# The end of FFN 1 in a one-layer encoder kernel: where weight copies, a table load, one tile's transposes and the next units stand

## The chip, the cores and the metric

The kernel runs on one core of one Trainium2 chip. A core has a matrix engine (TensorE, PE in the profile, with its weight loads as PEld), a vector engine (VectorE, DVE), a scalar engine (ScalarE, ACT), a general engine (GpSimd, POOL) and a queue engine (SyncE, SP); each works through its own list of instructions in order and waits on semaphores for the others. Data lies in SBUF, matmul results in PSUM banks, and 16 DMA engines move data from and to HBM.

The metric is the device time of one execution in microseconds (us). Before the change it is 1108.87 us, the median of three runs from 1108.83 to 1109.03.

## The reference

The reference computes one layer of a streaming encoder on 512 tokens of width 1024, in float32:

```python
h = x
f = swiglu(rms_norm(h, ffn1_pre_g), ffn1_w1, ffn1_w3, ffn1_w2)   # (silu(x@w1) * (x@w3)) @ w2, D_FF = 2816
h = h + 0.5 * rms_norm(f, ffn1_post_g)
u = rms_norm(h, mix_pre_g)
q, k, v, xr, xg = split(u @ w_in)                 # xr: 1024 columns
hr = rg_lru(causal_conv(xr))                      # gated linear recurrence over the tokens
y_a = (hr * gelu(xg)) @ w_lru_out
y_b = swa_sink_attention(q, k, v) @ w_attn_out    # windowed attention
g = sigmoid(u @ w_gate + b_gate)
h = h + rms_norm((g_a * y_a + g_b * y_b) @ w_o, mix_post_g)
h = h + 0.5 * rms_norm(swiglu(rms_norm(h, ffn2_pre_g), ffn2_w1, ffn2_w3, ffn2_w2), ffn2_post_g)
```

What matters here is the passage from the second line to the fifth: the end of FFN 1's last product, the norm of its result (post norm), the addition to `h`, the norm ahead of the mixer (pre norm), and the first products of `u` with the columns called `xr`.

## The kernel before

**Precision and matmuls.** Float32 products are made of three matmuls on split numbers: each operand is a high part (`whi`, a rounded copy) and a low part (`wlo`, the rest), and a product is high·high + high·low + low·high. So each weight tile of 128 x 1024 has to be copied (high part) and subtracted (low part) before PE can use it. For some weights, `xr` 0 to 3 among them, the low part is made by a DMA instead: ScalarE writes the negated high part (`wlo`, a second copy) and GpSimd issues a DMA that adds the weight from HBM to it. `dma_split(k, 0)` makes the first copy, `dma_split(k, 1)` the second and the DMA; `split_to` does both at once. `dma_to(n)` issues the plain loads (`raw_xr`) on SP's queue. Every instruction of an engine runs in the order in which the program writes it.

**The buffers.** All of these tiles come from one pool of 42 slots of 4 KB a partition; a new tile gets a slot that an older one has left, and its first writer waits for the older tile's last reader. PSUM has 8 banks, handed out in the same way.

**FFN 1's second product.** `tok_gemm` (called with `pre=half`) computes hidden @ w2 for four token tiles t = 0 to 3 of 128 tokens and two column halves n. Most of it is done by block products with sums of blocks (class `Halves`): seven products `m1, m5, m2, m6, m3, m7, m4` of five units each, 35 units u = 0 to 34 (`G` is 5). A unit has 12 matmuls of 512 columns, six for each token half. `step(u)` first prepares the operands of units up to u + 4 (`prep`: a ScalarE copy and a VectorE subtraction for the weight block at L686 and L694, the same for the hidden block at L226 and L227), then runs the unit's hooks, then issues its matmuls. At the end of `m7` (unit 29), VectorE adds the bank to a tile (L727), and only then may `m4` (units 30 to 34) go on in that bank. Two remaining rows of blocks (`TAIL_A`) are done as plain products, `classical(t, n)`, six matmuls each.

**The norms.** `norm(t, mid)` is post norm, addition and pre norm of one token tile: a chain between VectorE and ScalarE. VectorE adds the parts (L307) and scales (L310), ScalarE squares and sums (L309), the reciprocal root is taken on ScalarE with one correction on VectorE (L272 to L277), VectorE adds to `h` (L321), ScalarE squares again (L333), another root, and both engines scale one half of the result `hg` each (L344, L345). What `mid` issues stands between the first root and the second squares. After it, `transpose_mm` turns the tile by eight PE transposes (L354), and `transpose_out` writes its high part (ScalarE, L364) and low part (VectorE, L366) to `uT`, the operand of the next products. `transpose_xf` makes a float32 copy (L374) that is used later.

**The order at the end.** Units 0 to 24; tails of tiles 0 and 1; preparation to unit 31; norm 0; units 25 to 29 and the tails' column half 1 of tiles 2 and 3; preparation of units 33 and 34; norm 1; then, for tile 2: units 30 to 34 for token half 0, transposes of tile 0, the tail of tile 2, norm 2; for tile 3: units 30 to 34 for half 1, transposes of tile 1, the tail of tile 3. Then the first four units of the next product (`xr` 0 to 3, `bs[0]` to `bs[3]`): their first 256 tokens need tiles 0 and 1 alone, so `start` issues matmuls of 256 columns on those while norm 3 and the transposes of tiles 2 and 3 are made; the other 256 tokens come after that. Half of `bs[3]` is done with 512 columns at once.

**What stands in the hooks.** `X_AT` gives the units at which the plain loads of `xr` 0 to 3 are issued; the copies of `xr` 0 and 1 follow two units after their loads (`split_to`, ScalarE L159 and L160, GpSimd L161), those of `xr` 2 and 3 stand in the middles of norms 0, 1 and 2 (L169, L172, L174). `MARKS_A` gives the units for the loads and splits of the tails' weights and for the loads of `h` (L756, SP). `KEPT_AT` gives the units of three leftover gated products: scaling at units 15 and 16, `silu` at 18 and 19, product at 19 and 20. A root of a small tile is taken on ScalarE at unit 17 (`4 * G - 3`), so that the root's activation table is loaded there (L436). Each norm stores its `h` tile to HBM on SP's queue (L341).

Of the kernel before, what the change touches and what calls it, by code (L numbers as in the profile page):

```python
# [18 lines left out]
KT = D // P  # L19
# [32 lines left out]
def hybrid_layer(ctx: ExitStack, tc: tile.TileContext, a: dict, out: bass.AP):  # L52
# [111 lines left out]
    def dma_split(k, part):  # L164
        assert k == st["split"]
        if part == 0:
            dma_to(k + 1)
            half_split[k] = slot([P, D], F32R, name="whi"), slot([P, D], F32R, name="wlo")
            act.activation(half_split[k][0], raws[k], AF.Copy)  # L169
# [4 lines left out]
        pool.dma_start(out=lo, in_=a[nm][i * P : (i + 1) * P, :], accum_op=ALU.add)  # L174
        st["split"] += 1

    def split_to(n):
        while st["split"] < min(n, len(order)) and st["split"] not in paired:
            k = st["split"]
            dma_to(k + 1)  # L180
            r = raws.pop(k)
            if order[k] in BY_DMA:
                nm, i = order[k]
                pairs[k] = split_dma(r, a[nm][i * P : (i + 1) * P, :])
            else:
                hi = slot([P, D], F32R, name="whi")
                lo = slot([P, D], F32R, name="wlo")
                if order[k] in BY_POOL:
                    pool.tensor_copy(hi, r)
                else:  # L190
                    act.activation(hi, r, AF.Copy)
                dve.tensor_tensor(out=lo, in0=r, in1=f32(hi), op=ALU.subtract)
                pairs[k] = (hi, lo)
            st["split"] += 1
# [153 lines left out]
    def transpose_mm(hg):  # L348
        banks = []
        for half in range(2):  # L350
            ps = bank("tr")
            for k in range(4):
                kk = half * 4 + k
                pe.transpose(ps[:, k * P : (k + 1) * P], hg[:, kk * P : (kk + 1) * P], ident)  # L354
            banks.append(ps)
        return banks
# [20 lines left out]
    def tok_gemm(nm, xs, n, R, gpost_name, scale, gpre_name, first, x_to=None, xf=None, spill=False, then=None, eps=None, pre=None):  # L377
# [47 lines left out]
        def classical(t, n_):  # L425
            for k in tail:
                new = k == tail[0] and (t > 1 and n_ == 1 if pre else k == 0)
                mm_tok(accs(t), xs[k], t, w[k], new, k == tail[-1], (n_,), bool(pre))

        def norm(t, mid=None):  # L430
            us[t] = norms(acc[t], t, g[0], scale, g[1], spill, ep(t), mid, pre and pre.part(t), (1, 0) if pre and t > 1 else (0, 1))

        if pre:
            G = pre.G
            pre.hooks[3 * G].append(vectors)
            pre.hooks[4 * G - 3].append(lambda: act.activation(small(1, "tiny"), veps[:, 0:1], AF.Abs_reciprocal_sqrt))  # L436
# [24 lines left out]
            norm(1, lambda: [dma_split(x0 + 2, 1), dma_split(x0 + 3, 0)])  # L461
            for t in range(2, 4):
                for u in range(6 * G, 7 * G):
                    pre.step(u, (t - 2,))
                trs[t - 2] = transpose_mm(us[t - 2])
                transpose_out(trs[t - 2], t - 2, xf if t == 2 else None)
                classical(t, 0)
                if t == 2:
                    norm(2, lambda: dma_split(x0 + 3, 1))
            pre.bank.clear()  # L470
        else:
            tails()
            vectors()
            split_to(st["get"] + len(first))
            dma_to(st["split"] + 2)
            for t in range(NT):
                for n_ in range(2):
                    classical(t, n_)
                if t == NT - 1:
                    break  # L480
                if t >= 1:
                    trs[t - 1] = transpose_mm(us[t - 1])
                if t == NT - 2:
                    transpose_out(trs[t - 1], t - 1)
                norm(t)
                if t == 1:
                    transpose_out(trs[t - 1], t - 1, xf)
# [30 lines left out]
        k0, k1 = range(KT // 2), range(KT // 2, KT)  # L518
        whole = 3 if pre else 2
        mm_feat(bs[2], ws[2], 0, 256, ks=range(early, KT if pre else KT // 2))  # L520
        start(k0)
        get_ahead()
        for i in range(whole):
            mm_feat(bs[i], ws[i], 256, 512)
        if pre:
            point()
        mm_feat(bs[whole], ws[whole], 256, 512, ks=k0)
        if pre:
            point()
        mm_feat(bs[whole], ws[whole], ks=k1)  # L530
        if not pre:
            mm_feat(bs[3], ws[3])
        return bs

# [1393 lines left out]
```

## Time and profile before

| | |
|---|---|
| median of three runs | 1108.87 us (1108.83 to 1109.03) |
| the profiled execution, whole | 1109.03 us |
| its span, first to last instruction | 1107.2 us |
| PE busy in the span | 1092.7 us (99%) |
| DVE busy | 936.5 us (85%) |
| ACT busy | 700.8 us (63%) |
| POOL busy | 406.6 us (37%) |
| mean granted PE clock | 0.997 |

How to read the profile: it is one execution, with times in us from the first instruction of the span. A row of a timeline has start, duration, engine, line of the kernel, operation, `out<-in` by the program's tile names, shapes and a count; in brackets stands how long the engine was idle before it and what ended that wait. The wait table has, for an engine and line and what it waited for: us in total, times, longest. In the table of stretches each engine has its busy time and instructions, then come the granted PE clock (1.00 is full), the busy share of the DMA engines and GB/s. Matmuls are pipelined, so the end of one is later than the start of the next; I use distances from start to start. Queue engines have a `q` behind their name.

### The profile page before, as it was taken

The numbers are of one execution on the slowest core, as the hardware profiler recorded it, in microseconds if no ns is written. First come the engines' busy times: TensorE is split into PE (matmuls) and PEld (weight loads), VectorE is DVE, ScalarE is ACT, GpSimd is POOL, SyncE is SP. The second block draws the span as 40 slices with busy tenths as digits, with TensorE's granted clock in tenths as the row PEclk, the third lists the DMA queues.
The fourth block names the chain that finished last, engine by engine and source line by source line (L and its number), as shares of the span: only waits on it lengthen the run. The fifth ranks groups of instructions, "written<-read, shape, count | busy, mean of one in ns | idle before, by whom it ended". The sixth has DMA issues, their size and how long they took to land.

```text
span 1107.2 us, 18059 instructions
## 1 busy us (share of the span) xinstructions
PE 1092.7 (99%) x6850; PEld 987.9 (89%) x6850; DVE 936.5 (85%) x1328; ACT 700.8 (63%) x1211; POOL 406.6 (37%) x338
## 2 busy tenths in 40 slices
PE   9999999999989999999999999999999999999997
PEld 7899999988868877899888888888999999998886
DVE  5988999989888998888677867767789989999995
ACT  7756555598867687756656564456555555567672
POOL 0144923233001523223556564010877656521000
PEclk9999999999999999999999999999999999999999
DMA  9335653389856653147222245342423323547642
GB/s 337 121 84 138 136 142 115 124 180 203 244 144 189 179 127 114 41 148 251 78 76 85 90 170 209 127 183 81 143 76 115 102 90 111 195 149 187 179 120 90
DMA packets 53479, 156.99 MB, mean 142 GB/s; under 512 B 5504, under 2 KB 7424, under 8 KB 53392
## 3 DMA queue, kind: packets, MB, share of 16 engines
q1 hardware_dynamic: 43280, 129.57, 34.5%
q0 software_dynamic: 9824, 25.74, 12.2%
q8 instruction: 54, 0.88, 0.3%
q10 hardware_dynamic: 288, 0.52, 0.1%
q14 instruction: 33, 0.27, 0.1%
HBM read 137.99 MB, written 13.62 MB: 137 GB/s over the span
## 4 chain that ended last, share of the span: by engine, by line
PE 96%; DVE 1%; ACT 1%; issue 0%; DMA 0%; DVEq 0%; ACTq 0%
PE c L833 13%; PE c L834 13%; PE c L835 13%; PE f L237 10%; PE f L239 9%; PE f L238 9%; PE hw L717 5%; PE hw L715 5%; PE hw L716 5%; PE acc L255 1%; PE acc L256 1%; PE acc L257 1%; PE pt L1687 1%; PE s L1651 1%; PE s L1650 1%; PE o L1703 1%
## 5 line engine op out<-in xcount | busy, mean ns | idle before, releaser
L834 PE MATMUL c<-uT,wlo 128*128 128x256 f32 x516 | 146.1, 283 | 0.0
L835 PE MATMUL c<-uT,whi 128*128 128x256 f32 x516 | 146.1, 283 | 0.0
L833 PE MATMUL c<-uT,whi 128*128 128x256 f32 x516 | 146.1, 283 | 0.0
L833 PE MATMUL c<-Xh,whi 128*128 128x256 f32 x504 | 142.8, 283 | 0.0
L834 PE MATMUL c<-Xh,wlo 128*128 128x256 f32 x504 | 142.7, 283 | 0.0
L237 PE MATMUL f<-uT,whi 128*128 128x512 f32 (+1 forms) x376 | 138.0, 367 | 1.8 <-ACT uT L364 1.8
L239 PE MATMUL f<-uT,whi 128*128 128x512 f32 (+1 forms) x376 | 136.3, 363 | 0.2 <-DVE uT L366 0.2
L238 PE MATMUL f<-uT,wlo 128*128 128x512 f32 (+1 forms) x376 | 136.3, 362 | 0.0
L835 PE MATMUL c<-Xl,whi 128*128 128x256 f32 x456 | 129.1, 283 | 0.0
L227 DVE TENSOR_TENSOR wlo<-S,whi 128x1024 fp32r<-128x1024 f32 x86 | 121.0, 1408 | 5.9 <-POOL OL L1723 3.1
L226 ACT ACTIVATE whi<-S 128x1024 fp32r<-128x1024 f32 x86 | 88.5, 1054 | 29.7 <-DVE S L882 28.0
L833 PEld LDWEIGHTS c<-uT,whi 128*128 128x128 f32 x516 | 99.1, 192 | 0.2
L834 PEld LDWEIGHTS c<-uT,wlo 128*128 128x128 f32 x516 | 99.1, 192 | 0.2
L835 PEld LDWEIGHTS c<-uT,whi 128*128 128x128 f32 x516 | 99.1, 192 | 0.0
L833 PEld LDWEIGHTS c<-Xh,whi 128*128 128x128 f32 x504 | 96.8, 192 | 0.3 <-issue 0.3
L834 PEld LDWEIGHTS c<-Xh,wlo 128*128 128x128 f32 x504 | 96.8, 192 | 0.0
L717 PE MATMUL hw<-whi,uT 128*128 128x512 f32 x228 | 88.8, 390 | 0.0
L715 PE MATMUL hw<-whi,uT 128*128 128x512 f32 x228 | 88.7, 389 | 0.0
L716 PE MATMUL hw<-wlo,uT 128*128 128x512 f32 x228 | 88.7, 389 | 0.0
L835 PEld LDWEIGHTS c<-Xl,whi 128*128 128x128 f32 x456 | 87.6, 192 | 0.0
L237 PEld LDWEIGHTS f<-uT,whi 128*128 128x128 f32 x376 | 71.0, 189 | 14.4 <-ACT uT L364 2.2
L239 PEld LDWEIGHTS f<-uT,whi 128*128 128x128 f32 x376 | 70.9, 189 | 11.5 <-DVE uT L366 0.4
(441 smaller groups left out, 3193.7 us busy)
## 6 DMA issues: line engine op xcount, KB each, us to landing
raw_w2b<-in_w2b_dram SPq DMA_DIRECT2D x27, 512.0 KB, 4.6
raw_w1b<-in_w1b_dram SPq DMA_DIRECT2D x22, 512.0 KB, 4.2
raw_w3b<-in_w3b_dram SPq DMA_DIRECT2D x22, 512.0 KB, 4.4
raw_w3a<-in_w3a_dram SPq DMA_DIRECT2D x21, 512.0 KB, 4.7
raw_w1a<-in_w1a_dram SPq DMA_DIRECT2D x20, 512.0 KB, 4.3
raw_w2a<-in_w2a_dram SPq DMA_DIRECT2D x17, 512.0 KB, 8.3
raw_wg<-in_wg_dram SPq DMA_DIRECT2D x16, 512.0 KB, 4.0
raw_w2a<-in_w2a_dram POOLq DMA_DIRECT2D x15, 512.0 KB, 9.9
```

The lines of the kernel that those rows point to most:

```text
L226: act.activation(hi, src, AF.Copy)
L227: dve.tensor_tensor(out=lo, in0=src, in1=f32(hi), op=ALU.subtract)
L237: pe.matmul(ps[:, c0:c1], wh[:, s], h_, start=k == 0 and c0 == 0, stop=False, skip_group_check=True)
L238: pe.matmul(ps[:, c0:c1], wl[:, s], h_, start=False, stop=False, skip_group_check=True)
L239: pe.matmul(ps[:, c0:c1], wh[:, s], l_, start=False, stop=k == KT - 1, skip_group_check=True)
L255: pe.matmul(acc[n], x[:, 0, c], wh[:, s], start=first, stop=False, skip_group_check=skip)
L715: pe.matmul(ps, xs[:, 0, j, c], hi[:, j, :], start=start and j == 0, stop=False, skip_group_check=True)
L716: pe.matmul(ps, xs[:, 0, j, c], lo[:, j, :], start=False, stop=False, skip_group_check=True)
L717: pe.matmul(ps, xs[:, 1, j, c], hi[:, j, :], start=False, stop=i == self.G - 1, skip_group_check=True)
L833: pe.matmul(ps, wh[:, s], xh, start=first, stop=False, skip_group_check=True)
L834: pe.matmul(ps, wl[:, s], xh, start=False, stop=False, skip_group_check=True)
L835: pe.matmul(ps, wh[:, s], xl, start=False, stop=k == 3, skip_group_check=True)
```

## The change

It does five things at FFN 1's end; the second call of `tok_gemm` (without `pre`) keeps its order.

1. The copies of `xr` 0 and 1 leave the hooks. All copies of `xr` 0 to 3 are now issued around the norms: `xr` 0 (both copies) between the preparations and norm 0, `xr` 1 in the middle of norm 0, `xr` 2 between the preparations and norm 1, `xr` 3 with one copy in the middle of norm 1 and one in that of norm 2. All four low parts go by `dma_split`.
2. The plain loads of `xr` 0 to 2 are issued at units 22, 24 and 26 instead of 20, 21 and 24; that of `xr` 3 stays at 28.
3. The small root is taken at unit 22 (`4 * G + 2`), behind the last `silu` of unit 19, and not at unit 17.
4. After the transposes of tile 0 and the tail of tile 2, only unit 30 of token half 1 is done before the transposes of tile 1; then comes norm 2, and units 31 to 34 of half 1 and tile 3's tail follow. The float32 copies of tile 0 stand ahead of norm 2, those of tile 1 in its middle and behind it.
5. The first unit `bs[0]` is done whole for its first 256 tokens ahead of tile 2's transposes, `bs[1]` and `bs[2]` between those and tile 3's, `bs[3]` behind them; the second 256 tokens follow for all four, so that no matmul of these units has 512 columns.

```diff
-            pre.hooks[4 * G - 3].append(lambda: act.activation(small(1, "tiny"), veps[:, 0:1], AF.Abs_reciprocal_sqrt))
+            pre.hooks[4 * G + 2].append(lambda: act.activation(small(1, "tiny"), veps[:, 0:1], AF.Abs_reciprocal_sqrt))
...
             for i, u in enumerate(X_AT):
                 pre.hooks[u].append(lambda i=i: dma_to(x0 + i + 1))
-                if i < 2:
-                    pre.hooks[u + 2].append(lambda i=i: split_to(x0 + i + 1))
+
+            def x_split(i, parts=(0, 1)):
+                for p in parts:
+                    dma_split(x0 + i, p)
+
...
             pre.prep(5 * G + LEAD + 2)
-            norm(0, lambda: dma_split(x0 + 2, 0))
+            x_split(0)
+            norm(0, lambda: x_split(1))
...
-            norm(1, lambda: [dma_split(x0 + 2, 1), dma_split(x0 + 3, 0)])
-            for t in range(2, 4):
-                for u in range(6 * G, 7 * G):
-                    pre.step(u, (t - 2,))
-                trs[t - 2] = transpose_mm(us[t - 2])
-                transpose_out(trs[t - 2], t - 2, xf if t == 2 else None)
-                classical(t, 0)
-                if t == 2:
-                    norm(2, lambda: dma_split(x0 + 3, 1))
+            x_split(2)
+            norm(1, lambda: x_split(3, (0,)))
+            for u in range(6 * G, 7 * G):
+                pre.step(u, (0,))
+            trs[0] = transpose_mm(us[0])
+            transpose_out(trs[0], 0)
+            classical(2, 0)
+            pre.step(6 * G, (1,))
+            trs[1] = transpose_mm(us[1])
+            transpose_out(trs[1], 1)
+            transpose_xf(trs[0], 0, xf)
+            norm(2, lambda: [x_split(3, (1,)), transpose_xf(trs[1], 1, xf, (0,))])
+            transpose_xf(trs[1], 1, xf, (1,))
+            for u in range(6 * G + 1, 7 * G):
+                pre.step(u, (1,))
+            classical(3, 0)
...
         def between():
             transpose_out(trs[t - 1], t - 1, parts=(0,))
-            transpose_xf(trs[t - 2], t - 2, xf, (0,))
+            if not pre:
+                transpose_xf(trs[t - 2], t - 2, xf, (0,))
...
-        start(range(3))
-        trs[t - 1] = transpose_mm(us[t - 1])
-        mm_feat(bs[0], ws[0], 0, 256, ks=range(3, KT))
-        norm(t, between)
-        transpose_out(trs[t - 1], t - 1, parts=(1,))
-        transpose_xf(trs[t - 2], t - 2, xf, (1,))
-        start()
-        early = 5 if pre else 1
-        start(range(early))
+        if pre:
+            start()
+            trs[t - 1] = transpose_mm(us[t - 1])
+            norm(t, between)
+            transpose_out(trs[t - 1], t - 1, parts=(1,))
+            start()
+            start()
+        else:
...
-        mm_feat(bs[2], ws[2], 0, 256, ks=range(early, KT if pre else KT // 2))
-        start(k0)
+        if not pre:
+            mm_feat(bs[2], ws[2], 0, 256, ks=k0[1:])
+        start()
         get_ahead()
-        for i in range(whole):
-            mm_feat(bs[i], ws[i], 256, 512)
+        mm_feat(bs[0], ws[0], 256, 512)
+        mm_feat(bs[1], ws[1], 256, 512)
+        mm_feat(bs[2], ws[2], 256, 512, ks=k0)
         if pre:
+            mm_feat(bs[2], ws[2], 256, 512, ks=k1)
             point()
-        mm_feat(bs[whole], ws[whole], 256, 512, ks=k0)
-        if pre:
-            point()
-        mm_feat(bs[whole], ws[whole], ks=k1)
-        if not pre:
+            for ks in (k0, k1):
+                mm_feat(bs[3], ws[3], 256, 512, ks=ks)
+                point()
+        else:
+            mm_feat(bs[2], ws[2], ks=k1)
             mm_feat(bs[3], ws[3])
...
-X_AT = (20, 21, 24, 28)
+X_AT = (22, 24, 26, 28)
```

More of the change, by code (lines that the diff above doesn't have):

```diff
@@ L500, in between @@
             transpose_out(trs[t - 1], t - 1, parts=(0,))
-            transpose_xf(trs[t - 2], t - 2, xf, (0,))
-        start(range(3))
-        trs[t - 1] = transpose_mm(us[t - 1])
-        mm_feat(bs[0], ws[0], 0, 256, ks=range(3, KT))
-        norm(t, between)
-        transpose_out(trs[t - 1], t - 1, parts=(1,))
-        transpose_xf(trs[t - 2], t - 2, xf, (1,))
-        start()
-        early = 5 if pre else 1
-        start(range(early))
+            if not pre:
+                transpose_xf(trs[t - 2], t - 2, xf, (0,))
+        k0, k1 = range(KT // 2), range(KT // 2, KT)
+        if pre:
[6 more added lines that the diff above has]
+        else:
+            start(range(3))
+            trs[t - 1] = transpose_mm(us[t - 1])
+            mm_feat(bs[0], ws[0], 0, 256, ks=range(3, KT))
+            norm(t, between)
+            transpose_out(trs[t - 1], t - 1, parts=(1,))
+            transpose_xf(trs[t - 2], t - 2, xf, (1,))
+            start()
+            start(range(1))
         trs[t] = transpose_mm(us[t])
@@ L517, in tok_gemm @@
             then()
-        k0, k1 = range(KT // 2), range(KT // 2, KT)
-        whole = 3 if pre else 2
-        mm_feat(bs[2], ws[2], 0, 256, ks=range(early, KT if pre else KT // 2))
-        start(k0)
+        if not pre:
+            mm_feat(bs[2], ws[2], 0, 256, ks=k0[1:])
+        start()
         get_ahead()
-        for i in range(whole):
-            mm_feat(bs[i], ws[i], 256, 512)
+        mm_feat(bs[0], ws[0], 256, 512)
+        mm_feat(bs[1], ws[1], 256, 512)
+        mm_feat(bs[2], ws[2], 256, 512, ks=k0)
         if pre:
+            mm_feat(bs[2], ws[2], 256, 512, ks=k1)
             point()
-        mm_feat(bs[whole], ws[whole], 256, 512, ks=k0)
-        if pre:
-            point()
-        mm_feat(bs[whole], ws[whole], ks=k1)
-        if not pre:
+            for ks in (k0, k1):
[3 more added lines that the diff above has]
+            mm_feat(bs[2], ws[2], ks=k1)
             mm_feat(bs[3], ws[3])
```

## The prediction

> **What bounds the kernel now.** I read the page's first part, then who waited for whom on TensorE, then a table of stretches, then the timelines of each engine around FFN 1's end.
>
> ```profile
> PE 1092.7 (99%) x6850; PEld 987.9 (89%) x6850; DVE 936.5 (85%) x1328; ACT 700.8 (63%) x1211; POOL 406.6 (37%) x338
> ```
>
> TensorE (PE) is the bound: of a span of 1107.2 us it lacks 14.5. A change that takes no matmul away can win only waits, and this one works at the two largest.
>
> ```profile
> PE hw L715 <- DVE hc L727: 4.1, 1, 4.1
> PE f L237 <- ACT uT L364: 1.8, 1, 1.8
> ...
> 320.00:330.00 10.00, 5.92 (x20) 4.43 (x19) 8.70 (x15) 6.36 (x12) 0.00 (x0) 0.83 0.74 264
> ...
> 340.00:350.00 10.00, 7.99 (x45) 6.48 (x44) 8.48 (x20) 6.79 (x17) 3.67 (x5) 1.00 0.57 138
> ```
>
> The last two rows are stretches: PE's busy time comes first, the granted clock is the third number from the end. Both waits lie at FFN 1's end, and in the first one's stretch the clock is 0.83, in the second's 1.00. PE's timeline (start, duration):
>
> ```profile
> 321.72 0.39 PE L257 MATMUL acc<-whi,hT 128*128 128x512 f32 x1
> 326.18 0.47 PE L715 MATMUL hw<-whi,hx 128*128 128x512 f32 x1 [4.08 <-DVE hc L727]
> ...
> 327.26 0.63 PE L715 MATMUL hw<-whi,hx 128*128 128x512 f32 x1
> ...
> 329.82 0.48 PE L715 MATMUL hw<-whi,hx 128*128 128x512 f32 x1
> ...
> 330.60 0.39 PE L715 MATMUL hw<-whi,hx 128*128 128x512 f32 x1
> ...
> 334.69 1.03 PE L354 MATMUL tr<-ident,hg 128*128 128x128 f32 x8
> ...
> 347.93 0.39 PE L237 MATMUL f<-uT,whi 128*128 128x256 f32 x1 [1.79 <-ACT uT L364]
> ...
> 356.94 1.03 PE L354 MATMUL tr<-ident,hg 128*128 128x128 f32 x8
> 357.73 0.36 PE L237 MATMUL f<-uT,whi 128*128 128x256 f32 x1
> ...
> 370.40 0.40 PE L237 MATMUL f<-uT,whi 128*128 128x512 f32 x1
> ...
> 373.14 0.39 PE L237 MATMUL f<-uT,whi 128*128 128x512 f32 x1
> ```
>
> 330.60 to 334.69 are 18 matmuls of 512 columns: 0.227 us each. 357.73 to 370.40 are 105 of 256: 0.1207 each. 370.40 to 373.14 are 12 of 512: 0.228 each; at 373.14 the unit after the changed stretch begins, and it is my finishing line. Eight transposes take 0.79 (356.94 to 357.73). After the 4.08 us wait the spacing is 0.427 (six from 327.26 to 329.82); 326.18 to 330.60 hold 12 matmuls in 4.42, 1.70 more than at 0.227. So the first wait costs 4.2 + 1.7.
>
> From 321.95 (321.72 + 0.23) to the line PE has 72 matmuls of 0.227 (units 30 to 34 and the two tails), four times 0.79, 168 of 0.1207 and 12 of 0.228: 16.3 + 3.2 + 20.3 + 2.7 = 42.5. It took 51.2. **8.7 us** are lost here: all there is to win.
>
> **Why PE waits.** ScalarE (ACT) first, then VectorE (DVE).
>
> ```profile
> 280.00 1.28 ACT L436 ACT_TABLE_LOAD   x1
> ...
> 283.00 1.28 ACT L1356 ACT_TABLE_LOAD   x1
> ...
> 300.16 1.06 ACT L159 ACTIVATE whi<-raw_xr 128x1024 fp32r<-128x1024 f32 x1 [1.14 <-PE hw L716]
> ...
> 316.59 1.28 ACT L272 ACT_TABLE_LOAD   x1
> ...
> 318.09 1.05 ACT L169 ACTIVATE whi<-raw_xr 128x1024 fp32r<-128x1024 f32 x1
> ...
> 321.91 0.72 ACT L345 ACTIVATE hg<-hg,r 128x512 f32<-128x512 f32 x1 [0.63 <-DVE r L277]
> ...
> 326.42 0.61 ACT L226 ACTIVATE hx<-hEO 128x512 fp32r<-128x512 f32 x1
> ...
> 337.54 0.73 ACT L345 ACTIVATE hg<-hg,r 128x512 f32<-128x512 f32 x1 [0.63 <-DVE r L277]
> ```
>
> ```profile
> 303.15 1.23 DVE L694 TENSOR_TENSOR wlo<-raw_w2a,whi 128x1024 fp32r<-128x1024 f32 x1 [2.87 <-ACT whi L686]
> ...
> 306.51 1.23 DVE L694 TENSOR_TENSOR wlo<-raw_w2a,whi 128x1024 fp32r<-128x1024 f32 x1 [1.53 <-ACT whi L686]
> ...
> 313.47 0.68 DVE L307 TENSOR_TENSOR hc<-hw,hc 128x512 f32<-128x512 f32 x1
> ...
> 325.35 1.28 DVE L727 TENSOR_TENSOR hc<-hw,hc 128x512 f32<-128x512 f32 x2
> ...
> 330.02 0.69 DVE L307 TENSOR_TENSOR hc<-hw,hc 128x512 f32<-128x512 f32 x1
> ...
> 338.78 1.29 DVE L366 TENSOR_TENSOR uT<-tr,uT 128x512 fp32r<-128x512 f32 x2 [0.49 <-ACT uT L364]
> 339.99 0.68 DVE L307 TENSOR_TENSOR hc<-acc,hc 128x512 f32<-128x512 f32 x1
> ...
> 349.12 0.68 DVE L307 TENSOR_TENSOR hc<-acc,hc 128x512 f32<-128x512 f32 x1
> ...
> 355.75 0.75 DVE L344 SCALAR_TENSOR_TENSOR hg<-h,r,bc_mix_pre_g 128x512 f32<-128x512 f32 x1
> ...
> 361.59 5.47 DVE L192 TENSOR_TENSOR wlo<-raw_xr,whi 128x1024 fp32r<-128x1024 f32 x2 [2.10 <-ACT whi L191]
> ```
>
> Unit 30 waits for L727, which empties its bank. L727 stands on DVE behind unit 32's preparation, that behind norm 0 (313.47 to 321.91 + 0.72 = 322.63), and norm 0 behind preparations 27 to 31, which DVE could not feed: it stood still for 2.87 and 1.53 while ACT copied xr 0 and 1 (four copies of about a microsecond from 300.16, after 1.14 on a slot). Inside norm 0 lies a table load.
>
> **The change, part by part.** Times below are estimates from these rows.
>
> *Copies of xr 0 and 1, root table.* Four copies leave the hooks of units 22 and 23; one table load with its tiny operation comes to unit 22 instead. The two loads at 280.00 and 283.00 go (root, then silu again); PE had no wait there, so I cost them at nothing. DVE's 4.40 of waits fall but for some 0.3 behind the load: norm 0 starts at about 309.4. The two copies of xr 0 stand in ACT's queue before it and may hold its first ACT operation by up to half a microsecond; I take 0.3. Norm 0 took 9.16; it loses the 1.28 of the load, and its middle now holds two copies where 318.09 is one: between 0 (hidden under DVE's two halves) and +0.95; I take 0.4. It ends at 309.4 + 0.3 + 8.3 = 318.0, not 322.63.
>
> *Unit 30.* L727 began 2.72 after norm 0's end and PE 0.83 after L727's start: 321.55, under the 321.95 at which PE is free. The first wait goes, and with it the slow clock: −5.9. If norm 0 ends later than 318.4, PE waits for each microsecond of it.
>
> *Norm 1.* It began 7.39 after norm 0's end: 325.4. Its middle has one copy instead of two; it took 8.25 (330.02 to 337.54 + 0.73 = 338.27), norm 3 took 7.38 (349.12 to 356.50); I take 7.9: end 333.3.
>
> *Tile 1's transposes ahead of norm 2.* PE's order becomes five units for tile 0, transposes, tail, one unit for tile 1, transposes of tile 1: 321.95 + 42 × 0.227 + 0.79 = 332.3. Norm 1 ends at 333.3, so here comes a **new wait of 1.0** (bounds 0 and 2.0, from the spread of the terms above). Behind it stand four units, a tail and the first 24 half-matmuls. The wait of 1.79 at 347.93 goes, since uT of tile 1 is written long before.
>
> *Norms 2 and 3.* Norm 2 began 1.72 after norm 1's end, behind one tile's L366 pair; now behind two, +1.29: 336.3, end (7.38 again) 343.7. PE is there at 333.4 + 0.79 + 30 × 0.227 + 24 × 0.1207 = 343.9: no wait. Norm 3 follows at once and ends at 351.1; PE has 0.79 + 48 × 0.1207 more and is there at 350.5: **wait 0.6** (0 to 0.9). Before, 54 half-matmuls and a later start covered it.
>
> *Token halves.* Twelve matmuls of 512 columns become 24 of 256: 12 × (2 × 0.1207 − 0.228) = +0.16. By the Trainium skill, "TensorE: Matmul & The Clock Gate", section "Wait — 56ns, not 53.3ns?", one more matmul costs only about 2.5 ns, an estimate of 0.03; the rows say 13 ns, and they stay.
>
> *Queues.*
>
> ```profile
> 320.21 0.33 SPq L341 DMA_DIRECT2D h_scr<-h  x1
> ...
> 343.57 0.85 POOL L174 DMA_DIRECT2D wlo<-in_xr_dram  x1 [8.02 <-DVE r L277]
> ...
> raw_xr<-in_xr_dram SPq DMA_DIRECT2D x8, 512.0 KB, 5.6
> ...
> wlo<-in_xr_dram POOLq DMA_DIRECT2D x4, 512.0 KB, 6.8
> ```
>
> The raw loads of xr 0 to 2 come two, three and two units later on SP. But the copies move further than the loads: xr 0's load by two units (24 matmuls, 5.4 us), its copy from 300.16 to about 308; xr 1's load by three (8.2), its copy by about 9, into norm 0. Xr 2 now stands behind norm 0's store (320.21, then about 315.5) and lands some 6 later, at 321.5. ACT copies it after preparations 32 to 34, which ran 4.4 past norm 0's end (326.42 + 0.61): about 322.4, and norm 1 starts 3.0 after that, so 1.9 for two copies fits. POOL issues the four accumulating loads alone; xr 3's came 3.6 after norm 2's start, so at 339.9, lands by 346.7, is used at 351.9. Each copy costs at most 0.95 in its norm if the cover goes.
>
> *Behind it.* Xr 4 and 5 are ready at 367.1 (361.59 + 5.47) for 373.14. They move with norm 3's end (356.5 to 351.1); PE moves by 6.9, so 4.5 of the 6.0 remain.
>
> **Sum.** 8.7 lost before; after, 1.0 + 0.6 + 0.16 = 1.8. Gain **6.9**. The profiled execution took 1109.03 (1107.2 span, 1.8 around it): 1102.1; the median of the runs is 0.16 lower: **1102.0**.
>
> **Rivals.** *A, half the gain:* DVE stays unfed (slots, the table load in the hook, the copies of xr 0 before norm 0) and norm 0 ends only 1.7 earlier. PE then waits 2.5 at unit 30, 1.4 at tile 1, 0.6 at norm 3: with the halves 4.7 lost, gain 4.0, **1105.0**. For it: ACT did wait for slots (1.14). Whether 2.5 also slows the clock no row shows (1.79 didn't, 4.08 did), so 0 to 1.7 more, up to 1106.7. By the Trainium skill (same page, "Part 1: The HAM clock gate") PE drops to half rate after an idle window of about 3.4 us and needs as much work to return; both rows agree (0.427 until 329.82), and by it A keeps 1105.0.
>
> *B, no effect in the main:* norm 0 ends as before, since the load and copies only change places. The first wait stays with its slow clock (5.9), tile 1's transposes find norm 1 done, 0.6 and 0.16 come: gain 2.0, **1107.0**, within the bound. Against it: the 2.87 and 1.53 name ACT, which sheds four copies.
>
> *C, slower:* the copy of xr 2 stands ahead of norm 1 in ACT's queue, and its load behind norm 0's store in SP's. If it lands late, norm 1 waits, and tile 1's transposes hold PE with all units behind. Norm 1's first ACT operation follows its first addition, at 325.4 + 0.7 = 326.1, and the two copies need 1.9: each microsecond past 324.2 is one at PE, and a wait like the 4.08 adds 1.7 for the clock. The 6.9 are gone when it lands at 324.2 + 6.9 − 1.7 = 329.4; at 332.3, three landing times of 5.6 after norm 0's store, the loss is 8.1 + 1.7 and the time **1111.8**. Against it: 5.6 is the median.
>
> **How the numbers follow.** As forecast (1100.5 to 1103.6: no new wait at all, or tile 1's at 2.0 and norm 3's at 0.9 with 0.3 at unit 30) 0.67; A 0.16; B 0.07; C 0.08; 0.02 for some other gain. The range takes in the forecast and A: from 1100.3 (8.5 won, 0.2 of spread) to 1106.0. About 0.2% (2.2 us) is what can be told from no change: faster is the forecast, A and the rest, 0.85; same is B, 0.07; slower is C, 0.08.
>
> **What would show it.** Right: no wait of PE on L727, no stretch under clock 1.00 at 320 to 330, one table load instead of three between 280 and 320, norm 0's L307 near 309.4, waits of about 1.0 before tile 1's transposes and 0.6 before tile 3's, the next unit's first matmul near 366.2. Wrong: ACT waiting for raw_xr or a slot before norm 0 or 1, or a PE wait over 3 us at tile 1's transposes.

## The result and the profile after

The changed kernel takes **1102.45 us** (median, 1102.21 to 1102.58) against 1108.95 (1108.83 to 1109.36) for the kernel before: 6.5 us less, a ratio of 0.994 with a 95% interval of 0.9923 to 0.9958. The forecast was 1102.0, with a range of 1100.3 to 1106.0. The profiled execution took 1102.58 us, with a span of 1100.8.

The page's first part, PE's waits and the stretches of the changed kernel (columns as before; lines behind the edits are 21 higher than before, so L727 is now L748 and L686 is L707):

```profile
PE 1091.1 (99%) x6862; PEld 987.3 (90%) x6862; DVE 936.2 (85%) x1328; ACT 697.3 (63%) x1209; POOL 406.8 (37%) x338
```

```profile
PE tr L354 <- DVE hg L344: 1.2, 2, 1.0
...
320.00:330.00 10.00, 10.00 (x50) 8.38 (x49) 9.18 (x17) 6.84 (x12) 0.85 (x1) 1.00 0.91 282
330.00:340.00 10.00, 9.00 (x44) 7.27 (x43) 8.57 (x20) 8.19 (x20) 0.00 (x0) 1.00 0.27 82
```

Both old waits are gone. PE is busy through 320 to 330, where it had 5.92 of 10, and the clock there is 1.00 instead of 0.83. What is left is a wait for norm 1 at tile 1's transposes and a short one for norm 3 at tile 3's. PE's busy time changed by 1.6 us and its idle time from 14.5 to 9.7: the rest of the gain is the half-speed stretch, which counted as busy.

PE's timeline, then ScalarE's and VectorE's:

```profile
321.81 0.39 PE L257 MATMUL acc<-whi,hT 128*128 128x512 f32 x1
322.04 0.39 PE L736 MATMUL hw<-whi,hx 128*128 128x512 f32 x1
...
333.62 1.09 PE L354 MATMUL tr<-ident,hg 128*128 128x128 f32 x8 [1.00 <-DVE hg L344]
...
351.26 1.06 PE L354 MATMUL tr<-ident,hg 128*128 128x128 f32 x8 [0.22 <-DVE hg L344]
352.08 0.36 PE L237 MATMUL f<-uT,whi 128*128 128x256 f32 x1
...
366.56 0.40 PE L237 MATMUL f<-uT,whi 128*128 128x512 f32 x1
```

```profile
298.48 1.28 ACT L436 ACT_TABLE_LOAD   x1
...
324.56 1.06 ACT L169 ACTIVATE whi<-raw_xr 128x1024 fp32r<-128x1024 f32 x1 [2.25 <-DMA raw_xr<-in_xr_dram]
325.53 1.04 ACT L172 ACTIVATE wlo<-raw_xr 128x1024 fp32r<-128x1024 f32 x1
326.47 0.61 ACT L309 ACTIVATE junk<-hc 128x512 f32<-128x512 f32 x1
```

```profile
309.66 0.69 DVE L307 TENSOR_TENSOR hc<-hw,hc 128x512 f32<-128x512 f32 x1
...
317.18 0.75 DVE L344 SCALAR_TENSOR_TENSOR hg<-h,r,bc_mix_pre_g 128x512 f32<-128x512 f32 x1
...
320.63 1.28 DVE L748 TENSOR_TENSOR hc<-hw,hc 128x512 f32<-128x512 f32 x2
...
325.30 0.69 DVE L307 TENSOR_TENSOR hc<-hw,hc 128x512 f32<-128x512 f32 x1
...
332.81 0.75 DVE L344 SCALAR_TENSOR_TENSOR hg<-h,r,bc_mix_pre_g 128x512 f32<-128x512 f32 x1
...
336.45 0.68 DVE L307 TENSOR_TENSOR hc<-acc,hc 128x512 f32<-128x512 f32 x1
...
350.37 0.75 DVE L344 SCALAR_TENSOR_TENSOR hg<-h,r,bc_mix_pre_g 128x512 f32<-128x512 f32 x1
```

Unit 30 follows the tails with no gap (321.81, 322.04). The unit behind the changed stretch starts at 366.56 instead of 373.14, 6.58 earlier; with that the whole gain is made, and no later PE wait above 0.15 us came in its place. One thing in ScalarE's rows was not forecast: it stood still for 2.25 us waiting for xr 2's raw load, and norm 1's first operation came at 326.47, behind the two copies.

### The profile page after: what moved, and what is told of

It reads as the page before. It is cut to its first block, busy times and chain, and to the rows that moved or that the text cites. A ratio compares the mean times of both kernels' runs of the same rounds, so it can differ in the third digit from the quotient of the medians.

```text
span 1100.8 us, 18082 instructions
## 1 busy us (share of the span) xinstructions
PE 1091.1 (99%) x6862; PEld 987.3 (90%) x6862; DVE 936.2 (85%) x1328; ACT 697.3 (63%) x1209; POOL 406.8 (37%) x338
## 4 chain that ended last, share of the span: by engine, by line
PE 92%; ACT 2%; DVE 2%; DMA 2%; issue 1%; DVEq 0%; SPq 0%; ACTq 0%
PE c L854 13%; PE c L855 13%; PE c L856 13%; PE f L237 9%; PE f L239 9%; PE f L238 9%; PE hw L737 4%; PE hw L738 4%; PE hw L736 4%; PE acc L257 1%; PE acc L255 1%; PE acc L256 1%; PE pt L1708 1%; DMA raw_w2a<-in_w2a_dram 1%; DMA raw_xr<-in_xr_dram 1%
```

## Two theories and the experiments

The prediction priced PE's first wait and the slow clock after it as a gain of their own. That is one theory: **PE's own time counts**; a wait taken away and a clock kept up are gained where they happen. The other came up on reading the two traces side by side: **the chain of norms paces PE**. Norms 0 to 3, with the preparations and copies that stand between them, follow one another almost without a pause on VectorE and ScalarE; PE only fills the time between, and what it gains in one place it waits in the next, until the chain itself gets shorter. For the whole change both come to about the same time; they differ for its parts. All times below are medians, with their ranges; the kernel before was run beside each of the three sets of runs, at 1109.16, 1109.22 and 1109.27. The copies without the root, and the moved float32 copies of item 4 without the rest of it, were not run alone.

One caution for comparing single traces: a profiled execution can be late from the start. Each loses a different amount in the first 50 us of the span, and is late by that when the changed stretch begins: one and the same PE matmul ahead of it stands between 282.76 and 285.16 in the fourteen traces. Where it matters I count from that matmul (282.96 in the kernel before, 283.05 in the changed one) to the finishing line: **90.2** before, **83.5** for the change, and 83.7 for the change in a second trace.

### The copies, the loads and the root alone

The kernel before with the first three items of the change and the old order of transposes and units.

```diff
-            pre.hooks[4 * G - 3].append(...Abs_reciprocal_sqrt)
+            pre.hooks[4 * G + 2].append(...Abs_reciprocal_sqrt)
...
-            norm(0, lambda: dma_split(x0 + 2, 0))
+            x_split(0)
+            norm(0, lambda: x_split(1))
...
-            norm(1, lambda: [dma_split(x0 + 2, 1), dma_split(x0 + 3, 0)])
+            x_split(2)
+            norm(1, lambda: x_split(3, (0,)))
...
-                    norm(2, lambda: dma_split(x0 + 3, 1))
+                    norm(2, lambda: x_split(3, (1,)))
...
-X_AT = (20, 21, 24, 28)
+X_AT = (22, 24, 26, 28)
```

> The kernel before with the copies, the raw loads and the root table moved as in the change; transposes and next units in the old order. Theory (the chain of norms paces PE): unit 30 no longer waits and the clock stays at 1.00, but PE then stands at the first matmul of the next units, which need tile 1 behind norm 2: from about 340.0 to 343.2, a wait of 3.2 instead of 1.79. The next unit starts at 368.3 instead of 373.14: 1104.1 us. Rival (the first wait and its slow clock are simply won): 5.9 gained, 1103.0. If a wait of 3.2 already slows the clock: some 1105.8.

1106.62 us (1105.02 to 1108.59), ratio 0.9975 (0.9966 to 0.9985): 2.5 won, not 5.9. PE's waits and four stretches of the profiled execution, the one of 1108.59 us:

```profile
PE f L237 <- ACT uT L364: 3.0, 1, 3.0
...
344.99 0.58 PE L237 MATMUL f<-uT,whi 128*128 128x256 f32 x1 [2.97 <-ACT uT L364]
...
340.80:344.20 3.40, 1.21 (x6) 0.66 (x4) 3.04 (x8) 2.10 (x6) 3.40 (x5) 1.00 0.64 84
344.20:347.60 3.40, 2.62 (x11) 2.39 (x12) 2.85 (x5) 1.94 (x6) 0.11 (x1) 0.51 1.00 290
347.60:351.00 3.40, 3.40 (x18) 3.40 (x17) 2.82 (x7) 3.03 (x8) 0.00 (x0) 0.50 1.05 358
351.00:354.40 3.40, 3.40 (x30) 3.40 (x30) 3.09 (x9) 2.37 (x7) 0.00 (x0) 0.99 0.85 260
```

The first wait is gone, as expected, and the second has grown from 1.79 to 2.97, also as expected: PE comes early to the first matmul of the next units and has to wait for norm 2, behind which tile 1's transposes are written to `uT`. The rival, that the first wait is simply won, falls. The wait of 2.97 slows the clock too, here for two stretches of 3.4 us. This execution is also late from the start: the matmul from which I count stands at 284.76, 1.8 later than in the kernel before, so 1108.59 is not the slow clock's work alone. Counted from there, the first matmul of the next units comes 4.7 earlier than in the kernel before, as the chain's theory had it (343.2 for 347.93). From that matmul to the finishing line it then takes 27.6 instead of 25.2, since no wait for a norm lies behind it: here the 2.4 of the slow clock are lost for good, and 87.9 for 90.2 is what remains. The expectation had named this case, with 1105.8.

### The new order alone

The changed kernel with the first three items undone: root at unit 17, copies of xr 0 and 1 in the hooks, the old middles of the norms, the old `X_AT`.

```diff
...
-            x_split(0)
-            norm(0, lambda: x_split(1))
+            norm(0, lambda: dma_split(x0 + 2, 0))
...
-            x_split(2)
-            norm(1, lambda: x_split(3, (0,)))
+            norm(1, lambda: [dma_split(x0 + 2, 1), dma_split(x0 + 3, 0)])
...
-            norm(2, lambda: [x_split(3, (1,)), transpose_xf(trs[1], 1, xf, (0,))])
+            norm(2, lambda: [dma_split(x0 + 3, 1), transpose_xf(trs[1], 1, xf, (0,))])
...
```

> The kernel before with the new order of transposes and units alone; copies, raw loads and root as before. Theory: the first wait of 4.1 and the slow clock stay; tile 1's transposes find norm 1 about done, tile 3's wait some 0.5; the next unit starts near 371.2: gain 1.9, 1107.0 us (rival B of the prediction). Rival (the wait of 1.79 and nothing else goes): 1106.9, but without the wait at tile 3's transposes. Rival (the order is worth nothing without an earlier norm 1): 1108.9.

1107.34 us (1106.94 to 1109.6), ratio 0.9982 (0.9972 to 0.9991): 1.8 won, near the 2.0 of the prediction's rival B.

```profile
PE hw L731 <- DVE hc L743: 4.1, 1, 4.1
...
PE tr L354 <- DVE hg L344: 0.2, 1, 0.2
```

The first wait stays whole, the second is gone, and only 0.2 comes at the transposes. The two halves of the change give 2.5 and 1.8, the whole 6.5. The rest, 2.2, exists only with both; it is about the 2.4 that the slow clock costs in the first half, where the new order would have taken away the wait that brings it.

### The root's table load alone

```diff
-            pre.hooks[4 * G - 3].append(lambda: act.activation(small(1, "tiny"), veps[:, 0:1], AF.Abs_reciprocal_sqrt))
+            pre.hooks[4 * G + 2].append(lambda: act.activation(small(1, "tiny"), veps[:, 0:1], AF.Abs_reciprocal_sqrt))
```

> The kernel before with the root's table load moved alone. Norm 0 ends about 1.0 earlier, so unit 30 waits about 3.1 instead of 4.08. Does that still slow the clock? And does it matter? Theory (the chain of norms paces PE): whatever the clock does, the first matmul of the next units starts where norm 2 lets it, 1.0 earlier: gain 1.0, 1107.9 us; if the clock stays up, the wait there grows by about 1.7. Rival (PE's own time counts): the clock's 1.7 are won as well: gain 2.7, 1106.2 us.

1108.19 us (1107.95 to 1109.32), ratio 0.9988 (0.9978 to 0.9998): 0.97 won, where the chain's theory said 1.0 and PE's own time 2.7.

```profile
PE hw L715 <- DVE hc L727: 3.0, 1, 3.0
PE f L237 <- ACT uT L364: 0.6, 1, 0.6
...
321.00:324.40 3.40, 1.33 (x6) 0.75 (x4) 2.42 (x4) 3.33 (x5) 0.00 (x0) 1.00 1.03 316
324.40:327.80 3.40, 2.45 (x6) 2.00 (x7) 3.40 (x6) 1.79 (x3) 0.00 (x0) 0.50 0.91 364
327.80:331.20 3.40, 3.40 (x10) 2.63 (x9) 3.24 (x6) 0.72 (x2) 0.00 (x0) 0.50 0.01 5
331.20:334.60 3.40, 3.40 (x17) 2.79 (x16) 3.12 (x7) 3.00 (x6) 0.74 (x1) 1.00 0.00 0
```

This run decides between the theories for this place. The wait is a microsecond shorter, but the clock is at half for 6.8 us instead of 3.4, and still the kernel is 0.97 faster. PE lost more of its own time and it did not matter: it had 1.79 of waiting ahead of it at the next units, and has 0.6 now. In the kernel before, the slow clock was hidden behind norm 2.

### The root put back in the changed kernel

```diff
-            pre.hooks[4 * G + 2].append(...Abs_reciprocal_sqrt)
+            pre.hooks[4 * G - 3].append(...Abs_reciprocal_sqrt)
```

> The changed kernel with the small root back at unit 17. Theory: norm 0 holds the table load again (+1.28), starts some 0.36 earlier because the load no longer stands ahead of unit 27's preparation, and ends 0.9 later; every later norm moves by that, and PE waits about 0.35 at unit 30 and 1.5 at tile 1's transposes: 1103.35 us. Rival (the load hides): 1102.45.

1103.45 us (1103.22 to 1105.82), 1.0 slower than the change. The table load is back in norm 0, and tile 1's transposes wait 1.72 instead of 1.00:

```profile
321.52 0.39 PE L257 MATMUL acc<-whi,hT 128*128 128x512 f32 x1
321.99 0.47 PE L736 MATMUL hw<-whi,hx 128*128 128x512 f32 x1
...
334.41 1.09 PE L354 MATMUL tr<-ident,hg 128*128 128x128 f32 x8 [1.72 <-DVE hg L344]
```

Norm 0 started earlier here, at 308.91 instead of 309.66, and still ended later, at 318.47 instead of 317.93: with the 1.28 of the load inside it, it took 9.56 instead of 8.27. (Of the 0.75 by which it started earlier, 0.3 is there from the start of this execution.) Unit 30's first matmul now comes 0.47 behind the one before it, where the spacing is 0.227: a short wait for L748 behind norm 0. With what the next matmul loses it comes to 0.33, where 0.35 was expected. What is lost shows there and at tile 1's transposes, and as a microsecond of time, so the load inside a norm is on the path. That it could hide, the rival, falls. In this profile a wait of 1.72 left the clock at 1.00.

### Xr 2's raw load two units earlier

```diff
-X_AT = (22, 24, 26, 28)
+X_AT = (22, 24, 24, 28)
```

> The changed kernel with the raw load of xr 2 issued at unit 24 instead of 26, so that it stands ahead of norm 0's store on SP. Theory: the 2.25 us in which ScalarE waited for it go, norm 1's first ScalarE operation comes 0.45 earlier and norm 1 ends 0.45 earlier; PE's wait at tile 1's transposes falls from 1.0 to 0.55, and norms 2 and 3 follow: 1102.0 us. Rival (another slot is taken at norm 0 and something waits for one): no gain or a loss of up to 1.

1102.15 us (1101.77 to 1102.69), ratio 0.9937 (0.9924 to 0.9951). ScalarE's rows, as in the fence of the changed kernel above:

```profile
322.36 1.05 ACT L169 ACTIVATE whi<-raw_xr 128x1024 fp32r<-128x1024 f32 x1
...
326.23 0.63 ACT L309 ACTIVATE junk<-hc 128x512 f32<-128x512 f32 x1 [1.87 <-DVE hc L307]
```

The load is issued ahead of norm 0's store, ScalarE does not wait for it, and norm 1's first ScalarE operation waits for VectorE alone, as in the kernel before. The wait at tile 1's transposes falls from 1.00 to 0.69 (0.55 was expected). By the medians 0.3 is won, and by the traces 0.3 or 0.6 (83.2 from the same matmul to the line, for 83.5 and 83.7), but the ranges of the times overlap.

### Xr 2's raw load three units later

```diff
-X_AT = (22, 24, 26, 28)
+X_AT = (22, 24, 29, 29)
```

> The changed kernel with the raw loads of xr 2 and xr 3 issued at unit 29, behind the loads of h. This doubles the cause in rival C of the prediction: xr 2 lands some 1.5 to 2 us later than its 324.5, ScalarE waits for it ahead of norm 1, and PE's wait at tile 1's transposes grows by as much, to 2.5 to 3.0. Theory: each microsecond later is one at the end: 1104.0 to 1104.5 us. Rival (norm 1 has slack): 1102.45.

1108.1 us (1107.33 to 1110.2), ratio 0.9991 (0.9982 to 1.0). This edit makes what the prediction's rival C describes, and nearly the whole gain is gone. ScalarE's row, PE's wait, and four stretches of 3.4 us:

```profile
327.70 1.06 ACT L169 ACTIVATE whi<-raw_xr 128x1024 fp32r<-128x1024 f32 x1 [5.71 <-DMA raw_xr<-in_xr_dram]
```

```profile
PE tr L354 <- DVE hg L344: 4.8, 2, 4.4
```

```profile
330.60:334.00 3.40, 1.76 (x8) 1.13 (x6) 3.12 (x7) 2.34 (x5) 0.26 (x1) 1.00 0.70 101
334.00:337.40 3.40, 0.62 (x6) 0.62 (x7) 2.61 (x8) 2.74 (x8) 0.00 (x0) 1.00 0.65 207
337.40:340.80 3.40, 3.40 (x12) 2.83 (x11) 3.37 (x6) 2.80 (x6) 0.00 (x0) 0.50 0.00 0
340.80:344.20 3.40, 3.40 (x16) 2.78 (x16) 2.80 (x8) 2.83 (x8) 1.01 (x2) 0.99 0.00 0
```

The expectation missed the size, 1104.0 to 1104.5. The load landed 3.1 later than in the change, not 1.5 to 2, and the wait of 4.42 then slowed the clock for 3.4 us. Norm 3 ended 3.15 later than in the change (354.27), but the next unit began 4.36 later (370.92): behind the slow stretch PE came to tile 2's transposes at 349.03, when norm 2 had ended at 346.98. So here PE's own time, the slow clock with it, did count. Which of the two theories holds is a matter of the place: the one that is late there sets the end.

### One more unit ahead of tile 1's transposes

```diff
-            pre.step(6 * G, (1,))
+            for u in range(6 * G, 6 * G + 2):
+                pre.step(u, (1,))
             trs[1] = transpose_mm(us[1])
...
-            for u in range(6 * G + 1, 7 * G):
+            for u in range(6 * G + 2, 7 * G):
                 pre.step(u, (1,))
```

> The changed kernel with units 30 and 31 of token half 1, not 30 alone, ahead of tile 1's transposes. PE's wait of 1.0 there is filled with matmuls. Theory (the chain of norms paces PE): norm 2 and 3 end where they did, the wait moves to tile 2's transposes (0.4 to 0.9) and tile 3's, and nothing is won: 1102.4 us, at most 0.2 off. Rival (PE's own order counts): 1.0 won, 1101.5 us.

1103.16 us (1102.51 to 1103.28), ratio 0.9945 (0.9932 to 0.9957). The work put into the 1.00 of waiting took it away, and it came back 10 us later:

```profile
334.20 1.09 PE L354 MATMUL tr<-ident,hg 128*128 128x128 f32 x8
...
344.54 1.06 PE L354 MATMUL tr<-ident,hg 128*128 128x128 f32 x8 [0.88 <-DVE hg L344]
...
351.84 1.06 PE L354 MATMUL tr<-ident,hg 128*128 128x128 f32 x8 [0.48 <-DVE hg L344]
```

The rival, a gain of 1.0, falls: nothing is won. By the medians 0.6 to 0.7 is lost, against runs of another set, where the theory had said at most 0.2; the trace does not show such a loss. Tile 1's transposes do come 0.58 later than in the change (334.20 for 333.62), but so does norm 1's end, which they follow by 0.06 in both traces, and 0.49 of it is there at norm 0's start (310.15 for 309.66), ahead of the edit. Counted from the same matmul the line comes after 83.8, for the change's 83.5 and 83.7. What the medians lost stays open.

### The old order of the next units

The changed kernel with the next units in the order of the kernel before: three steps of the first unit ahead of tile 2's transposes, the rest of it, the second unit and five steps of the third ahead of tile 3's, and half of the fourth in 512 columns.

```diff
-            start()
+            start(range(3))
             trs[t - 1] = transpose_mm(us[t - 1])
+            mm_feat(bs[0], ws[0], 0, 256, ks=range(3, KT))
             norm(t, between)
...
             start()
-            start()
+            start(range(5))
...
-        if not pre:
-            mm_feat(bs[2], ws[2], 0, 256, ks=k0[1:])
-        start()
+        mm_feat(bs[2], ws[2], 0, 256, ks=range(5, KT) if pre else k0[1:])
+        start(k0 if pre else range(KT))
...
-            for ks in (k0, k1):
-                mm_feat(bs[3], ws[3], 256, 512, ks=ks)
-                point()
+            mm_feat(bs[3], ws[3], 256, 512, ks=k0)
+            point()
+            mm_feat(bs[3], ws[3], ks=k1)
```

> The changed kernel with the next units in their old order (three k-blocks of the first unit ahead of tile 2's transposes, the fourth unit half in 512 columns); all else as changed. Theory: PE reaches tile 2's transposes 15 half-matmuls (1.8 us) earlier and waits some 1.4 there for norm 2, the wait at tile 3's goes, fewer matmuls are done by then; the next unit starts 0.85 later: 1103.3 us. Rival (the halves only cost their extra 0.16): 1102.3 us.

1103.52 us (1102.87 to 1104.03), ratio 0.9946 (0.9934 to 0.9958). It ran beside the change itself:

> The changed kernel as it is, beside the other runs of this set: 1102.2 to 1102.7 us. It is the yardstick for the differences below one microsecond.

which took 1102.52 us (1102.34 to 1102.81), ratio 0.9937 (0.9924 to 0.9951). The new order of the units is worth 1.0. PE's waits of the two, the old order first:

```profile
344.11 1.06 PE L354 MATMUL tr<-ident,hg 128*128 128x128 f32 x8 [1.32 <-DVE hg L344]
...
351.49 1.04 PE L354 MATMUL tr<-ident,hg 128*128 128x128 f32 x8
```

```profile
344.44 1.04 PE L354 MATMUL tr<-ident,hg 128*128 128x128 f32 x8
...
351.42 1.06 PE L354 MATMUL tr<-ident,hg 128*128 128x128 f32 x8 [0.20 <-DVE hg L344]
```

With the old order PE comes to tile 2's transposes with less behind it and stands there for 1.32; with the new one for nothing, and 0.20 at tile 3's. The order spreads the matmuls over the two norms, a gain that the prediction did not price by itself: it gave the units a wait of 0.6 and a cost of 0.16.

### A shorter chain

Xr 2's load at unit 24 as above, and only one copy of xr 1 inside norm 0; the other goes behind it, ahead of xr 2's.

```diff
-            norm(0, lambda: x_split(1))
+            norm(0, lambda: x_split(1, (0,)))
...
+            x_split(1, (1,))
             x_split(2)
...
-X_AT = (22, 24, 26, 28)
+X_AT = (22, 24, 24, 28)
```

> The changed kernel with xr 2's raw load at unit 24, and the second copy of xr 1 taken out of norm 0's middle and put ahead of xr 2's copies, where ScalarE would then idle. Theory: norm 0 ends 0.45 earlier and norm 1 0.9 earlier; PE's waits at tile 1's and tile 3's transposes fall to about 0.3 each: 0.9 won, 1101.5 us. Rival (only the landing of xr 2 counts): 1102.0, as with the load alone.

1102.11 us (1101.67 to 1102.33), ratio 0.9936 (0.9924 to 0.9948): 0.04 less than with the early load alone, which ran beside it, so by the medians the rival holds. Its trace has the wait at tile 1's transposes where the theory put it, about 0.3:

```profile
333.31 1.09 PE L354 MATMUL tr<-ident,hg 128*128 128x128 f32 x8 [0.34 <-DVE hg L344]
```

Once more beside the change itself:

> The kernel with xr 2's load at unit 24 and the second copy of xr 1 behind norm 0, again, beside the changed kernel. Theory (the chain of norms paces PE; its profile had the stretch 0.66 shorter): 0.6 below the changed kernel. Rival (no difference that counts): within 0.2 of it.

1101.93 us (1101.61 to 1102.14), ratio 0.9932 (0.992 to 0.9945). Its slowest execution is faster than the change's fastest (1102.34), and the medians are 0.6 apart; its median is the lowest of this study.

```profile
333.31 1.09 PE L354 MATMUL tr<-ident,hg 128*128 128x128 f32 x8 [0.64 <-DVE hg L344]
```

Norm 1 ends at 333.25 where the change beside it has 333.72, and the wait is 0.64 for 1.24. Norm 0 did become some 0.37 shorter (310.08 to 317.99, against 309.69 to 317.97), but it also began 0.39 later, in both traces of this kernel, and ended where it did. The edit is not the reason. In the first trace the whole execution is 0.35 late from its first 50 us; counted from the same matmul, norm 0 ends 0.3 earlier than in the change and the line comes after 82.9. In the second, ScalarE and VectorE are some 0.3 to 0.4 late against PE from 292 on, ahead of anything that the edit moves, and the line comes after 83.2, as with the early load alone. So the gain over the change is shown, and by the medians it is that of xr 2's earlier load; whether the shorter norm adds its 0.3 in a usual run these five and five executions do not tell.

### Xr 2's raw load at unit 28

```diff
-X_AT = (22, 24, 26, 28)
+X_AT = (22, 24, 28, 28)
```

> The changed kernel with the raw load of xr 2 at unit 28 instead of 26, one transfer later in SP's queue. Between unit 26 (PE waits 1.0 at tile 1's transposes) and unit 29 (4.42, with half clock after it) this should give a wait of about 2 to 3. It asks whether such a wait slows the clock too. If it does not: each microsecond of wait is one at the end, 1103.7 to 1104.5 us. If it does, as the waits of 2.97 and 3.02 did: 1 to 3 us more, and a wider spread.

1106.17 us (1103.69 to 1108.41), ratio 0.9971 (0.9962 to 0.998). The wait at tile 1's transposes in the profiled execution (1105.91 us) was 3.39, longer than the 2 to 3 that this run was meant to try, since the raw load was waited for until 326.79. The time is within what was expected if the clock slows. The wait and the stretches around it:

```profile
335.84 1.89 PE L354 MATMUL tr<-ident,hg 128*128 128x128 f32 x8 [3.39 <-DVE hg L344]
...
332.60:336.00 3.40, 0.16 (x1) 0.16 (x2) 2.88 (x8) 2.64 (x7) 0.00 (x0) 1.00 0.78 233
336.00:339.40 3.40, 3.40 (x13) 3.02 (x13) 2.96 (x5) 2.90 (x6) 0.00 (x0) 0.50 0.00 0
```

So no run here has a wait between 1.8 and 2.9 us. The last section shows that the wait's length alone does not decide.

## Why the prediction was right, and where its steps were off

**The sum.** 6.9 was forecast and 6.5 measured. At the finishing line PE is at 366.56 instead of 366.2; the profiled execution took 1102.58 for a forecast of 1102.1, its median 1102.45 for 1102.0.

**Norm 0 and unit 30.** Norm 0 was put at 309.4 to 318.0 and ran from 309.66 to 317.93. Unit 30's bank was free when the tails were done. This step held, the root's term with it: putting the table load back makes norm 0 longer by the 1.28 of the sum (9.56 for 8.27) and costs 1.0 in all: norm 0 then also begins earlier, while xr 2's load, issued behind norm 0's store, comes later (316.57 for 316.05).

**Norm 1 and tile 1's transposes.** Start 325.4 forecast, 325.30 measured; wait 1.0 forecast, 1.00 measured. That they agree so well is in part luck: norm 1 took 8.26 instead of 7.9, and PE too came 0.3 later than worked out. The mis-sized term is **xr 2's landing**. "lands some 6 later, at 321.5" took the median of 5.6; the load was issued at 316.05, with three loads of `h` and xr 3's around it in SP's queue, and ScalarE had it at 324.56, 8.5 later. Its two copies then ended some 0.4 after norm 1's first ScalarE operation could have started. The early load (0.69 of wait instead of 1.00) and the late ones (3.39 and 4.42) bear this out from both sides.

**Norms 2 and 3.** Norm 2 was forecast from 336.3 to 343.7 and began at 336.45; PE met tile 2's transposes without a wait. Norm 3's end was forecast at 351.1 and came at 351.12. The wait there was 0.22, not 0.6, since PE came to it at 351.04, not 350.5.

**The halves.** From 352.08 to 366.56 are 120 matmuls of 256 columns, 0.1207 each with none of 512 among them; the term of 0.16 stands. By the Trainium skill, "TensorE: Matmul & The Clock Gate", section "Wait — 56ns, not 53.3ns?", it would be 0.03, an estimate; the trace here does not agree, its spacing of 0.1207 is that of the rows before.

**What was wrong in the working, though not in the sum.** "The first wait goes, and with it the slow clock: −5.9" reads as a term of its own. It is none. The first three items, which take this wait away, win 2.5; the root alone shortens the wait by 1.0 with twice the slow time and wins 0.97. In the kernel before, the slow clock only used up time in which PE would have waited for norm 2. The sum came out since it did not rest on that item: it took PE's whole way to the finishing line, with every new wait worked out from the norms' ends. Had one half of the change been judged by this item alone, the forecast would have been 3.4 us off (5.9 for 2.5).

**The rivals.** A, VectorE unfed, did not come about. B's result of 1107.0 is nearly what the new order alone gives (1107.34), for B's reason: the first wait stays. C's mechanism is real, as the late loads show. By its own rule a landing at 327.7 (324.2 + 3.5) would lose 3.5 and 1.7, for 1107.2; it measured 1108.1. Two units later, at 28, xr 2's load already costs 3.7. For A the prediction left open whether a wait of 2.5 slows the clock. By the Trainium skill, "TensorE: Matmul & The Clock Gate", section "Part 1: The HAM clock gate", it takes an idle window of about 3.4 us; here waits of 2.97 and 3.02, with PE busy 1.21 and 1.33 in the stretch of 3.4 us ahead of the slow ones, were enough, so the trace does not agree with an idle window of the full length.

## What to carry to other kernels

When the busiest engine waits in several places, first find what those waits have in common: here one chain of norms on two other engines, and a wait taken away in one place came back in the next until the chain itself began earlier and got shorter. Here the sum came out that followed PE to a line behind all the waits and worked each of them out anew; a single wait's row said little of what taking it away alone would win. Whether a slow clock costs anything depended on what stood behind it: nothing where PE had a wait ahead of it, 2.4 where it had none. When copies are moved into an engine's pauses, move their loads with an eye on the queue: a landing time from a quiet stretch does not hold where five large loads are issued together, and a late load ahead of the chain costs its delay and, once the wait takes enough of a window (last section), the clock.

## What the runs showed of the chip that I had not expected

A wait of 2.97 and one of 3.02 slowed PE's clock to 0.50, and for two stretches of 3.4 us each, though the waits of 3.39, 4.08 and 4.42 were longer and slowed it for one stretch. Waits of 1.72 and 1.79 did nothing. The traces' own record of the granted clock settles why. In the kernel before, the clock became full at 5.73, half at 326.58 and full again at 329.99: 94 and 95 times 3.413 us after the first. In the five other traces with a slow stretch, too, each change lies a whole number of 3.413 us after the first. So the clock was decided in windows of that length, which did not begin with the wait.

With PE's busy time counted by these windows, from each trace's first change on, all fourteen traces agree. A window with PE busy for 1.35 us or less was followed by half clock, one with 1.65 or more was not; at half clock, windows with 2.46 and 2.67 kept it, and one with 3.20 ended it. The first row of the fence of xr 2's late load shows it: 1.76 busy, and the clock stays at 1.00. The waits of 2.97 and 3.02 had taken most of one window and reached into the next, so that the next was not busy enough to end the slow time; the waits of 1.72 and 1.79 each lay across two windows. An estimate from these rows, 3.41 less 1.65 and less 1.35: a single wait of up to about 1.8 us does not slow the clock, and one above about 2.1 does if it falls into one window. What happens with 1.35 to 1.65 busy, and at half clock with 2.67 to 3.20, no trace shows.

The time of the kernels with such a wait varies as well: 3.6 us (1105.02 to 1108.59) and 4.7 us (1103.69 to 1108.41) over ten executions, against 0.5 over five for the change beside the last of them. That the clock is the reason is not shown: with the root put back the clock stayed full, and four executions differ by 2.6 us (1103.22 to 1105.82).
